# A hybrid S5 and gated-delta-rule layer on one core: a wide key norm, S5 setup queued behind the inputs, and the gate values computed later

## The chip, the cores and the metric

One core of a Trainium2 chip runs the whole layer in one launch. The metric is device time in microseconds, the median of several runs. The engines are TensorE (PE in the profile, its weight loads PEld), VectorE (DVE), ScalarE (ACT), GpSimd (POOL) and SyncE (SP), which issues most DMAs.

## The reference

One layer of a backbone on 1024 latent tokens and 256 context tokens, width 1024:

```
shift, scale, gate = split(silu(c) @ w_ada + b_ada)        # also for the context, from c_ctx
h = x * (1 + scale) + shift
u, z_s5, qkv, z_gdn, beta_l, alpha_l = split(h @ w_in)
S5 group (512 channels): diagonal complex state space, both directions, then GLU, times silu(z)
delta-rule group (4 heads of 128): q, k, v = silu(conv3x3(qkv)); q, k = l2norm(q), l2norm(k)
    beta = sigmoid(beta_l);  g = -exp(a_log) * softplus(alpha_l + dt_bias)
    chunked gated delta rule in both directions, gated RMS norm, times silu(z)
x_new = LN(alpha * x + gate * (concat(s5, gdn) @ w_out))
```

The key norm divides each key row of 128 by the root of its sum of squares plus 1e-6.

## The kernel before

The kernel is one long program; the framework takes the instructions in the order of the program as their priority, estimates when each is ready, and writes a fixed list for each engine. An instruction of low priority may so stand far ahead of its place in the program, in a hole of its engine. Each engine then runs its list in order, and a waiting instruction holds up what stands behind it. The block form `tc.issue_after(ins)` adds an edge from `ins` to the instructions in the block that are on the same engine as `ins`.

The front (`ada`, `hidden`, lines 509 to 572) goes over k = 0 to 7, the eight 128-wide slices of the width. `ada(k)` loads the x and context tiles and two 512 KB tiles `wad` of w_ada from SP's queue, and computes shift and scale (`pa`, `pas`, `ss`); `hidden(k)` transposes x on PE, scales it on ACT (`hraw`), splits it on DVE into `h_hi` and `h_lo`, and adds it to the u projection (`u_mm`). `s5_lam`, `s5_small` (line 240 on) compute powers of the S5 transition on small DVE tiles. `s5_load` (line 209) loads B, C (`bt`, `cnt`) and the skip weights into `spk`. `s5_mats` (line 370) forms the complex products of B, `s5_inject` (line 452) makes eight tiles `e` of products, three per tile on DVE and three on POOL for six of them, all six on DVE for two; PE transposes them, ACT copies them and they go to memory as `d_e`. `u_half` finishes the u projection in two halves. `e_stage` (line 613) loads `d_e` again and makes the chunk inputs `ebuf`; `fold` combines them on DVE, and `chain` is the sequential recurrence on POOL in three pieces, the second and third queued behind the key norm of heads 0 and 1 (`kpow`).

Between these stand, before the change, the values of beta and decay (`beta`, `lnb`, `gg`, `gx`, `ngx`): some 45 small DVE instructions, five on ACT and eight on PE. They are used first in `tbatch`, in the delta-rule part.

Then come four heads, each with three `conv_tile` calls (k, v, q): `proj` projects into PSUM banks of `psA` (four), ACT copies to `cr` and `ca`, DVE adds the taps, ACT applies SiLU, and for k and v PE transposes ten 128x128 blocks in groups of 4, 4 and 2 into PSUM banks of tag `w` (two banks; the function `bankE` gives the two of tag `e`). The buffers `ca` (tag `ac`) are two, shared by k, v and q. For k the groups are squared with a row sum on ACT (`jk`, `kss`), raised to -1/2 on POOL, multiplied on DVE into `ktk`, and transposed again (`pkT`). After head 1 stands `gate_stage`, which uses tag `e`. After the heads come the z projections, the S5 output, the GLU and the delta rule with the output projection.

Of the kernel before, what the change touches and what calls it, by code (L numbers as in the profile page):

```python
# [19 lines left out]
P = 128  # L20
# [21 lines left out]
def tile_hybrid_block(  # L42
# [462 lines left out]
    KS = 5  # L505
    pba = bankW("pba")
    xin = {}

    def ada(k):
        xk = hp.tile([P, 8, P], F32, tag=f"hh{k}", name=f"xk{k}")  # L510
        xc = hc.tile([P, 2, P], F32, tag=f"ch{k}", name=f"xc{k}")
        Q.dma_start(xk, x[0, :, k * P:(k + 1) * P].rearrange("(i p) f -> p i f", p=P))
        Q.dma_start(xc, cx[0, :, k * P:(k + 1) * P].rearrange("(i p) f -> p i f", p=P))
        wad = []
        for i in range(2):
            if k < 4:
                w = hp.tile([P, NK, P], F32, tag=f"h{'hl'[i]}{4 + k}", name=f"wad{k}_{i}")
            elif i:
                w = hp.tile([P, NK, P], F32, tag=f"hl{k}", name=f"wad{k}_{i}")
            else:  # L520
                w = c5([P, NK, P], f"wad{k}_{i}", ("kk", "ac")[k % 2])
            Q.dma_start(
                w, w_ada[0, :, i * D + k * P:i * D + (k + 1) * P].rearrange("(kt p) n -> p kt n", p=P),
            )
# [12 lines left out]
        pas = ld.tile([P, 256], F32, tag="pas", name=f"pas{k}", bufs=1)  # L537
        V.tensor_copy(pas, pa[:, :256])
        pm = pa[:, 256:260]
        for i in range(2):  # L540
            T.matmul(pm[:, 2 * i:2 * i + 2], pas[:, i * P:(i + 1) * P], sel, start=True, stop=True)
        ss = ld.tile([P, 4], F32, tag="ss", name=f"ss{k}")
        V.tensor_scalar(ss[:, 0:2], pm[:, 0:2], badd[:, k:k + 1], None, op0=ALU.add)
        V.tensor_scalar(ss[:, 2:4], pm[:, 2:4], badd[:, 8 + k:9 + k], 1.0, op0=ALU.add, op1=ALU.add)
        xin[k] = xk, xc, ss

    def hidden(k):
# [11 lines left out]
        h_hi[k] = hp.tile([P, LAT], F32R, tag=f"hh{k}", name=f"h_hi{k}")  # L559
        V.tensor_copy(h_hi[k], raw[:, :LAT])  # L560
        h_lo[k] = hp.tile([P, LAT], F32R, tag=f"hl{k}", name=f"h_lo{k}")
        V.tensor_tensor(h_lo[k], raw[:, :LAT], h_hi[k].bitcast(F32), op=ALU.subtract)  # L562
        c_hi[k] = hc.tile([P, CTX], F32R, tag=f"ch{k}", name=f"c_hi{k}")
        V.tensor_copy(c_hi[k], raw[:, LAT:])
        c_lo[k] = hc.tile([P, CTX], F32R, tag=f"cl{k}", name=f"c_lo{k}")
# [173 lines left out]
    def conv_tile(typ, hd):  # L739
# [44 lines left out]
        kt = c5([P, NT, P], "kt" + nm, "kk")  # L784
        if typ == 2:
            for i0, n4 in quads(NT):
                pv = bankW(f"pv{nm}_{i0}")
                for j in range(n4):
                    T.transpose(pv[:, j * P:(j + 1) * P], acc[:, (i0 + j) * P:(i0 + j + 1) * P], ident)
                S.activation(kt[:, i0:i0 + n4, :].rearrange("p j f -> p (j f)"), pv[:, :n4 * P], AF.Copy)  # L790
# [1 line left out]
            return  # L792
        kss = ld.tile([P, NT], F32, tag="kss", name=f"kss{hd}")
        for i0, n4 in quads(NT):
            pk = bankW(f"pk{nm}_{i0}")
            for j in range(n4):
                T.transpose(pk[:, j * P:(j + 1) * P], acc[:, (i0 + j) * P:(i0 + j + 1) * P], ident)
            for j in range(n4):
                jk = ld.tile([P, P], F32, tag="jk", name=f"jk{hd}_{i0}_{j}", bufs=1)
                S.activation(jk, pk[:, j * P:(j + 1) * P], AF.Square, accum_out=kss[:, i0 + j:i0 + j + 1])  # L800
            sl = slice(i0, i0 + n4)
            V.tensor_scalar(kss[:, sl], kss[:, sl], 1e-6, None, op0=ALU.add)  # L802
            kpow[hd] = G.tensor_tensor(kss[:, sl], kss[:, sl], mhalf[:, :n4], op=ALU.pow)  # L803
            V.tensor_tensor(
# [3 lines left out]
        S.dma_start(d_kt[hd], kt.rearrange("p j f -> p (j f)"))  # L808
        kT = c5([P, NT, P], "kT" + nm, "kk")
        for i0, n4 in quads(NT):  # L810
            pk = bankW(f"pkT{nm}_{i0}")
            for j in range(n4):
                T.transpose(pk[:, j * P:(j + 1) * P], kt[:, i0 + j, :], ident)
            S.activation(kT[:, i0:i0 + n4, :].rearrange("p j f -> p (j f)"), pk[:, :n4 * P], AF.Copy)
# [137 lines left out]
        for typ in (1, 2, 0):  # L952
            conv_tile(typ, hd)

    s5_load()
    bas = c5([P, 512], "bas", "kk")
    V.memset(bas, 0.0)
    for b, tn in enumerate((512, 512, 256)):
# [15 lines left out]
        for t in range(6):  # L974
            T.transpose(pcw[:, (6 * i + t) * 9:(6 * i + t + 1) * 9], cwn[:, t * P:(t + 1) * P], ident[:9, :9])
    V.tensor_copy(cwt.rearrange("p t a -> p (t a)"), pcw[:, :108])
    gr = per.tile([P, 2, 8], F32, name="gr")
    Q.dma_start(gr[:, 0, :], a_log.rearrange("o d h -> o (d h)").to_broadcast([P, 8]))
    Q.dma_start(gr[:, 1, :], dt_bias.rearrange("o d h -> o (d h)").to_broadcast([P, 8]))
    nea = sp.tile([P, 8], F32, name="nea")  # L980
    S.activation(nea, gr[:, 0, :], AF.Exp)
    V.tensor_scalar(nea, nea, -1.0, None, op0=ALU.mult)

    def gt(nm):
        return per.tile([P, 2, NT, HEADS], F32, name=nm)

    def dview(off):
        return gam[:, :, off:off + 8].rearrange("p n (d h) -> p d n h", d=2)

    def v4(t):  # L990
        return t.rearrange("p d n h -> p d (n h)")

    beta = gt("beta")
    for d in range(2):
        S.activation(beta[:, d], dview(0)[:, d], AF.Sigmoid)
    gtmp = ld.tile([P, 256], F32, tag="pas", name="gtmp", bufs=1)
    gtmq = ld.tile([P, P], F32, tag="jk", name="gtmq", bufs=1)
    ya, yb, yz = (gtmp[:, 80 * i:80 * i + 80].rearrange("p (d n h) -> p d n h", d=2, n=NT) for i in range(3))
    yq = gtmq[:, :80].rearrange("p (d n h) -> p d n h", d=2, n=NT)

    def softplus():
        V.tensor_scalar(yb, ya, -1.0, None, op0=ALU.mult)
        V.tensor_tensor(yb, ya, yb, op=ALU.min)
        S.activation(yb, yb, AF.Exp)
        V.tensor_scalar(yz, yb, 2.0, None, op0=ALU.add)
        V.reciprocal(yz, yz)
        V.tensor_mul(yz, yb, yz)
        V.tensor_mul(yb, yz, yz)
        V.tensor_scalar(yq, yb, 1.0 / 17, None, op0=ALU.mult)
        for cf in (1 / 15, 1 / 13, 1 / 11, 1 / 9, 1 / 7, 1 / 5, 1 / 3):  # L1010
            V.scalar_tensor_tensor(out=v4(yq), in0=v4(yq), scalar=cf, in1=v4(yb), op0=ALU.add, op1=ALU.mult)
        V.scalar_tensor_tensor(out=v4(yq), in0=v4(yq), scalar=1.0, in1=v4(yz), op0=ALU.add, op1=ALU.mult)
        V.tensor_scalar(ya, ya, 0.0, None, op0=ALU.max)
        V.scalar_tensor_tensor(out=v4(yq), in0=v4(yq), scalar=2.0, in1=v4(ya), op0=ALU.mult, op1=ALU.add)

    lnb = gt("lnb")
    for d in range(2):
        V.tensor_scalar(ya[:, d], dview(0)[:, d], -1.0, None, op0=ALU.mult)
    softplus()
    V.tensor_scalar(lnb, yq, -1.0, None, op0=ALU.mult)  # L1020
    for d in range(2):
        V.tensor_tensor(
            ya[:, d], dview(8)[:, d], bc(gr[:, 1, None, 4 * d:4 * d + 4], [P, NT, HEADS]), op=ALU.add,
        )
    softplus()
    gg = yb
    for d in range(2):
        V.tensor_tensor(gg[:, d], yq[:, d], bc(nea[:, None, 4 * d:4 * d + 4], [P, NT, HEADS]), op=ALU.mult)
    ghi = per.tile([P, 2, NT, HEADS], F32R, name="ghi")
    V.tensor_copy(ghi, gg)  # L1030
    ghf = ghi.bitcast(F32)
    glo = gt("glo")
    V.tensor_tensor(glo, gg, ghf, op=ALU.subtract)
    u_half(0)
    gx = per.tile([P, 2, 3, NT, HEADS], F32, name="gx")
    pgx = bankW("pgx")
    NC4 = NT * HEADS
    for d in range(2):
        for i, m in enumerate((tri[:, d, :], trir[:, d, :].bitcast(F32), ones)):
            o = (d * 3 + i) * NC4  # L1040
            T.matmul(pgx[:, o:o + NC4], m, gg[:, d].rearrange("p n h -> p (n h)"), start=True, stop=True)
    S.activation(gx.rearrange("p d i n h -> p (d i n h)"), pgx[:, :6 * NC4], AF.Exp)
    V.tensor_mul(gx[:, :, 1], beta, gx[:, :, 1])
    pgt = bankW("pgt")
    for d in range(2):
        T.transpose(pgt[:NC4, d * P:(d + 1) * P], gx[:, d, 0].rearrange("p n h -> p (n h)"), ident)
    grt = ld.tile([P, 256], F32, tag="pas", name="grt", bufs=1)
    V.tensor_copy(grt[:NC4], pgt[:NC4, :256])
    Q.dma_start(d_gr.rearrange("n h d p -> (n h) d p"), grt[:NC4].rearrange("p (d f) -> p d f", d=2))
    ngx = gt("ngx")  # L1050
    V.tensor_scalar(ngx, gx[:, :, 0], -1.0, None, op0=ALU.mult)
    s5_mats()
    s5_inject()
    u_half(1)
    pidx = sp.tile([P, 1], I32, name="pidx")
    G.iota(pidx, pattern=[[0, 1]], base=0, channel_multiplier=1)
# [621 lines left out]
```

## Time and profile before

| | us |
|---|---|
| median of 3 runs (range) | 923.16 (920.37 to 924.47) |
| profiled execution | 919.21 |
| its span | 917.5 |
| PE busy in the span | 814.1 (89%) |
| DVE busy | 672.5 (73%) |
| ACT busy | 415.2 (45%) |
| POOL busy | 392.1 (43%) |

The profile is one execution. Busy times count instructions in flight; PE's matmuls are pipelined, so that a busy PE isn't PE at its peak. The granted clock of PE is given beside it as a share of full speed, 0.949 over the span. An engine's idle time is put down to what ended it.

### The profile page before, as it was taken

The page shows a single profiled execution, that of the slowest core. Times are in us where ns is not written, and L with a number is a line of the kernel's source. Part 1 is how long each engine was busy: PE and PEld are TensorE (multiplying, and loading weights), DVE is VectorE, ACT ScalarE, POOL GpSimd, SP SyncE. Part 2 cuts the span into 40 slices and gives each one's busy share as a digit, 9 for nine tenths or more (in the row PEclk, how much of TensorE's full clock was granted, in tenths as well). Part 3 has the DMA queues.
Part 4 walks back from the last instruction along what each step waited for, and adds up shares of the span by engine and source line. Part 5 has one row for each costly group of instructions (what it writes and reads, how often), then busy time and mean ns, then how long its engine had stood idle before and what let it go on. Part 6 is the DMA issues. An engine that isn't in the chain of part 4 may idle for free. (4 is left out here: it accounts for less than half of the span.)

```text
span 917.5 us, 17187 instructions
## 1 busy us (share of the span) xinstructions
PE 814.1 (89%) x6553; PEld 674.8 (74%) x6553; DVE 672.5 (73%) x1318; ACT 415.2 (45%) x944; POOL 392.1 (43%) x463
## 2 busy tenths in 40 slices
PE   4988999997898999996899896899989889789994
PEld 2656897785786788874688674687988778678882
DVE  7988986996776778799573388567685585676686
ACT  1321435324434444431544376465763473556353
POOL 3215240007897940100311078874874485441163
PEclk9999999999798999998799897799999999999998
DMA  9981557412304232243454476421135234315332
GB/s 245 302 158 42 196 157 232 146 36 79 132 24 142 106 104 84 94 159 93 122 148 134 148 269 213 145 75 59 48 109 161 82 115 156 128 41 182 126 126 93
DMA packets 120125, 119.49 MB, mean 130 GB/s; under 512 B 21406, under 2 KB 95702, under 8 KB 119914
## 3 DMA queue, kind: packets, MB, share of 16 engines
q1 hardware_dynamic: 101946, 85.42, 32.7%
q10 hardware_dynamic: 18096, 32.97, 9.5%
q8 instruction: 51, 0.84, 0.4%
q14 instruction: 32, 0.26, 0.1%
HBM read 81.33 MB, written 37.04 MB: 129 GB/s over the span
## 5 line engine op out<-in xcount | busy, mean ns | idle before, releaser
L713 POOL TENSOR_TENSOR rta<-ebuf,ar 128x64 f32<-128x64 f32 x38 | 24.8, 653 | 85.3 <-DVE ebuf L688 82.6
L847 POOL COPY hq<-ebuf 64x1024 f32<-64x1024 f32 x8 | 16.4, 2068 | 93.9 <-DVE ebuf L688 58.5
L1187 POOL TENSOR_TENSOR mg<-tri,ghi 128x512 fp32r<-128x512 f32 x20 | 23.2, 1162 | 70.7 <-PE pd L1195 35.4
L1282 DVE TENSOR_TENSOR pad<-pp,lvm 128x256 f16<-128x256 f32 x100 | 40.5, 416 | 16.3 <-PE pp L1274 15.6
L141 PE MATMUL pjz<-h_hi,wtz 128*128 128x512 f32 x128 | 52.0, 406 | 0.1
L142 PE MATMUL pjz<-h_lo,wtz 128*128 128x512 f32 x128 | 52.0, 407 | 0.0
L143 PE MATMUL pjz<-h_hi,wtz 128*128 128x512 f32 x128 | 51.3, 401 | 0.0
L1298 PEld LDWEIGHTS <-xz 128*128 128x128 f16 x480 | 37.6, 101 | 18.5 <-issue 12.5
L1298 PE MATMUL px<-pad,xz 128*128 128x64 f16 x480 | 42.8, 198 | 7.0 <-DVE pad L1282 6.5
L1311 DVE TENSOR_TENSOR xz<-px,xz 128x512 f16<-128x512 f32 x60 | 40.6, 684 | 10.8 <-PE px L1298 8.8
L759 DVE SCALAR_TENSOR_TENSOR cak<-crk,cwt,cak 128x945 f32<-128x945 f32 (+2 forms) x32 | 39.3, 1229 | 7.3 <-ACT cak L749 6.9
L759 DVE SCALAR_TENSOR_TENSOR caq<-crq,cwt,caq 128x945 f32<-128x945 f32 (+2 forms) x32 | 39.2, 1224 | 7.2 <-ACT caq L749 5.3
L1298 PE MATMUL px<-xz,pad 128*128 128x64 f16 x480 | 42.8, 198 | 0.0
L759 DVE SCALAR_TENSOR_TENSOR cav<-crv,cwt,cav 128x945 f32<-128x945 f32 (+2 forms) x32 | 39.4, 1231 | 4.1 <-ACT cav L749 3.8
L1274 PE MATMUL pp<-xz,t 128*128 128x64 f16 x480 | 33.1, 197 | 7.1 <-DVE xz L1311 3.3
L803 POOL TENSOR_TENSOR kss<-kss,mhalf 128x4 f32<-128x4 f32 (+1 forms) x12 | 15.6, 1309 | 55.5 <-DVE kss L802 55.5
L1399 ACT ACTIVATE uu<-s 128x128 f32<-128x128 f32 x80 | 21.0, 275 | 38.7 <-PE s L1395 38.5
L1390 DVE SCALAR_TENSOR_TENSOR rr<-s,ngx,vt 128x128 f32<-128x128 f32 x72 | 24.5, 344 | 17.0 <-PE s L1386 16.4
L1274 PEld LDWEIGHTS <-t 128*128 128x128 f16 x480 | 27.5, 101 | 12.4 <-issue 10.4
L141 PE MATMUL u<-wu,h_lo 128*128 128x512 f32 x64 | 29.3, 458 | 5.5 <-DVE h_lo L562 5.5
L822 ACT ACTIVATE csz<-pjz 128x512 f32<-128x512 f32 x16 | 9.2, 597 | 54.9 <-PE pjz L143 43.0
L1395 PE MATMUL s<-rr,zf 128*128 128x128 f32 x144 | 31.4, 303 | 2.3 <-DVE rr L1390 1.8
(514 smaller groups left out, 3029.1 us busy)
## 6 DMA issues: line engine op xcount, KB each, us to landing
wad<-in_w_ada_dram SPq DMA_DIRECT2D x16, 512.0 KB, 6.3
xk<-in_x_dram SPq DMA_DIRECT2D x8, 512.0 KB, 6.5
d_e<-et ACTq DMA_DIRECT2D x8, 512.0 KB, 2.8
etl<-d_e SPq DMA_DIRECT2D x8, 512.0 KB, 4.3
wg<-in_w_ada_dram SPq DMA_DIRECT2D x8, 512.0 KB, 5.7
wrz<-in_w_in_dram SPq DMA_DIRECT2D x8, 512.0 KB, 3.9
d_z<-csz ACTq DMA_DIRECT2D x8, 512.0 KB, 2.9
xr<-in_x_dram SPq DMA_DIRECT2D x8, 512.0 KB, 5.4
```

What stands on the lines that cost most here:

```text
L141: T.matmul(ps, ll, rh, start=first, stop=False)
L142: T.matmul(ps, lh, rl, start=False, stop=False)
L143: return T.matmul(ps, lh, rh, start=False, stop=last)
L713: G.tensor_tensor(ta, prev, ar, op=ALU.mult)
L759: clast[typ, hd] = V.scalar_tensor_tensor(out=o, in0=rv[:, y0 + dy:y1 + dy, x0 + dx:x1 + dx], scalar=cwt[:, t, (dy + 1) * 3 + dx + 1:(dy + ...
L1187: G.tensor_tensor(mg[:, i], bc(tri[:, 0:2, None, :], [P, 2, 2, P]), bc(gsrc[:, :, c0:c0 + 2, hd, None], [P, 2, 2, P]), op=ALU.mult,)
L1274: T.matmul(pp[:, u * 64:(u + 1) * 64], t16[:, u, :], cols(xs[u], b, u // 2), start=True, stop=True)
L1282: V.tensor_tensor(scat(pad[:, 0, :], b, 256, 128 // b), pp[:, :256].rearrange("p (d n b) -> p d n b", d=2, b=b), lvm[:, l - 1].rearrange(" ...
L1298: ins = T.matmul(o, lt, rt, start=not on_act, stop=not on_act or w == 3 and i == 1)
L1311: V.tensor_tensor(xo, pxv, xo, op=ALU.add)
L1390: V.scalar_tensor_tensor(out=rn, in0=p1_[:, :P], scalar=ngx[:, d, ch, hd:hd + 1], in1=rr, op0=ALU.mult, op1=ALU.add,)
L1395: ins = T.matmul(p2_[:, :P], hs["zf"][cp][:, d, i, :], rr, start=True, stop=True)
```

## The change

Four edits. The loads of `s5_load` are queued on SP behind the last `wad` load. The DVE instructions of `s5_mats` and `s5_inject` are queued behind the last `h_lo`. The block that computes beta and decay stands after `head(1)` instead of before `s5_mats`; its text is the same, but `nea` is in another pool. In `conv_tile` the row sums of squares come from one ACT square over the whole group into `kt` and a DVE reduction, and the third group of each set of transposes takes a bank of tag `e`.

```diff
+            front["wad"] = Q.dma_start(w, w_ada[...])
...
+        front["lo"] = V.tensor_tensor(h_lo[k], raw[:, :LAT], h_hi[k].bitcast(F32), op=ALU.subtract)
...
-                pv = bankW(f"pv{nm}_{i0}")
+                pv = (bankE if i0 == 8 else bankW)(f"pv{nm}_{i0}")
...
-            pk = bankW(f"pk{nm}_{i0}")
+            pk = (bankE if i0 == 8 else bankW)(f"pk{nm}_{i0}")
...
-            for j in range(n4):
-                jk = ld.tile([P, P], F32, tag="jk", name=f"jk{hd}_{i0}_{j}", bufs=1)
-                S.activation(jk, pk[:, j * P:(j + 1) * P], AF.Square, accum_out=kss[:, i0 + j:i0 + j + 1])
             sl = slice(i0, i0 + n4)
+            S.activation(kt[:, sl, :].rearrange("p j f -> p (j f)"), pk[:, :n4 * P], AF.Square)
+            V.tensor_reduce(out=kss[:, sl], in_=kt[:, sl, :], axis=AX.X, op=ALU.add)
             V.tensor_scalar(kss[:, sl], kss[:, sl], 1e-6, None, op0=ALU.add)
...
-            pk = bankW(f"pkT{nm}_{i0}")
+            pk = (bankE if i0 == 8 else bankW)(f"pkT{nm}_{i0}")
...
-    s5_load()
+    with tc.issue_after(front["wad"].ins):
+        s5_load()
...
-    gr = per.tile([P, 2, 8], F32, name="gr")
...
     u_half(0)
-    s5_mats()
-    s5_inject()
+    with tc.issue_after(front["lo"].ins):
+        s5_mats()
+        s5_inject()
     u_half(1)
...
     for hd in range(HEADS):
         head(hd)
+        if hd == 1:
+            gr = per.tile([P, 2, 8], F32, name="gr")
...
         if hd < 2:
             with tc.issue_after(kpow[hd].ins):
```

## Rows read from the trace of the kernel before

**Rows 1.** Stages: busy (count) of PE, PEld, DVE, ACT, POOL, then PEclk, DMA, GB/s.
```profile
44.00:92.00 48.00, 40.56 (x286) 28.44 (x287) 40.87 (x92) 12.53 (x19) 17.39 (x12) 0.93 0.53 107
92.00:137.40 45.40, 45.40 (x240) 42.42 (x238) 40.15 (x89) 19.27 (x41) 16.68 (x11) 1.00 0.51 177
137.40:222.80 85.40, 83.60 (x579) 66.57 (x576) 74.63 (x105) 30.12 (x57) 11.00 (x14) 1.00 0.44 127
222.80:247.00 24.20, 15.40 (x82) 13.39 (x80) 13.09 (x15) 13.91 (x39) 19.47 (x36) 0.78 0.32 116
247.00:300.00 53.00, 49.09 (x237) 38.58 (x237) 36.90 (x39) 21.09 (x49) 45.45 (x71) 0.91 0.29 100
```

**Rows 2.** Waits of PE: who waited for whom, us in total, times, longest.
```profile
PE pkk L797 <- DVE ktk L804: 9.6, 2, 5.7
```

**Rows 3.** Timeline of SP's queue, 36 to 70 us: start, duration, what it issued.
```profile
44.98 5.55 SPq L213 DMA_DIRECT2D bt<-in_s_b_re_dram  x2
...
51.83 1.40 SPq L512 DMA_DIRECT2D xk<-in_x_dram  x1
...
66.09 0.38 SPq L512 DMA_DIRECT2D xk<-in_x_dram  x1
66.56 0.53 SPq L522 DMA_DIRECT2D wad<-in_w_ada_dram  x1
```

**Rows 4.** Timeline of DVE in the front.
```profile
76.27 1.77 DVE L407 TENSOR_TENSOR e<-e,e1v 128x512 f32<-128x512 f32 x1
77.97 2.12 DVE L562 TENSOR_TENSOR h_lo<-hraw,h_hi 128x1024 fp32r<-128x1024 f32 x1
80.01 1.77 DVE L406 TENSOR_TENSOR e2v<-spk,ep 128x512 f32<-128x512 f32 x1
81.70 0.41 DVE L538 COPY pas<-pa 128x256 f32<-128x256 f32 x1
```

**Rows 5.** Timeline of PE in the front (k = 5, then k = 7).
```profile
72.68 0.63 PE L142 MATMUL u<-wu,h_hi 128*128 128x512 f32 x1
...
88.73 0.60 PE L141 MATMUL u<-wu,h_lo 128*128 128x512 f32 x1
89.17 0.41 PE L142 MATMUL u<-wu,h_hi 128*128 128x512 f32 x1
```

**Rows 6.** Touching spk (DVE, POOL); POOL's products; last product; touching gtmp (PE, PEld, DVE, ACT).
```profile
44.00:88.25 44.25, 11.22 (x13) 10.74 (x9) 0.92 0.57 116
...
L408 POOL TENSOR_TENSOR e<-spk,ep 128x512 f32<-128x512 f32 x2 | 2.6, 1336 | 0.1
...
132.41 0.68 DVE L410 TENSOR_TENSOR e<-e,e7g 128x512 f32<-128x512 f32 x1
...
92.00:122.00 30.00, 1.43 (x12) 1.42 (x12) 13.77 (x42) 0.54 (x2) 1.00 0.52 181
```

**Rows 7.** The key norm: timelines of PE and POOL, then groups of ACT and DVE.
```profile
229.59 0.66 PE L797 MATMUL pkk<-ident,cak 128*128 128x128 f32 x2 [5.70 <-DVE ktk L804]
278.34 0.66 PE L797 MATMUL pkk<-ident,cak 128*128 128x128 f32 x2 [3.91 <-DVE ktk L804]
...
227.38 0.32 POOL L716 TENSOR_TENSOR ebuf<-rta,rtb 128x64 f32<-128x64 f32 x1
227.65 1.04 POOL L803 TENSOR_TENSOR kss<-kss,mhalf 128x4 f32<-128x4 f32 x1
276.45 2.00 POOL L803 TENSOR_TENSOR kss<-kss,mhalf 128x4 f32<-128x4 f32 x2
...
L800 ACT ACTIVATE jk<-pkk 128x128 f32<-128x128 f32 x40 | 11.1, 278 | 10.8 <-PE pkk L797 10.0
L800 ACT ACTIVATION_READ_ACCUMULATOR jk<-pkk 128x1 f32 x40 | 7.9, 198 | 0.0
L1004 ACT ACT_TABLE_LOAD x1 | 1.3, 1283 | 0.1
L804 DVE TENSOR_TENSOR ktk<-pkk,kss 128x512 f32<-128x512 f32 (+1 forms) x12 | 7.2, 600 | 13.3 <-POOL kss L803 13.3
```

More of the change, by code (lines that the diff above doesn't have):

```diff
@@ L507, in tile_hybrid_block @@
     xin = {}
+    front = {}
     def ada(k):
@@ L521, in ada @@
                 w = c5([P, NK, P], f"wad{k}_{i}", ("kk", "ac")[k % 2])
-            Q.dma_start(
+            front["wad"] = Q.dma_start(
                 w, w_ada[0, :, i * D + k * P:i * D + (k + 1) * P].rearrange("(kt p) n -> p kt n", p=P),
@@ L561, in hidden @@
         h_lo[k] = hp.tile([P, LAT], F32R, tag=f"hl{k}", name=f"h_lo{k}")
-        V.tensor_tensor(h_lo[k], raw[:, :LAT], h_hi[k].bitcast(F32), op=ALU.subtract)
+        front["lo"] = V.tensor_tensor(h_lo[k], raw[:, :LAT], h_hi[k].bitcast(F32), op=ALU.subtract)
         c_hi[k] = hc.tile([P, CTX], F32R, tag=f"ch{k}", name=f"c_hi{k}")
@@ L976, in tile_hybrid_block @@
     V.tensor_copy(cwt.rearrange("p t a -> p (t a)"), pcw[:, :108])
-    gr = per.tile([P, 2, 8], F32, name="gr")
[L978 to L1033, printed above, removed]
-    u_half(0)
[L1035 to L1049, printed above, removed]
@@ L1050, in tile_hybrid_block @@
-    ngx = gt("ngx")
-    V.tensor_scalar(ngx, gx[:, :, 0], -1.0, None, op0=ALU.mult)
-    s5_mats()
-    s5_inject()
+    u_half(0)
+    with tc.issue_after(front["lo"].ins):
+        s5_mats()
+        s5_inject()
     u_half(1)
@@ L1104, in tile_hybrid_block, with gt, dview, v4 @@
         head(hd)
+        if hd == 1:
+            gr = per.tile([P, 2, 8], F32, name="gr")
+            Q.dma_start(gr[:, 0, :], a_log.rearrange("o d h -> o (d h)").to_broadcast([P, 8]))
+            Q.dma_start(gr[:, 1, :], dt_bias.rearrange("o d h -> o (d h)").to_broadcast([P, 8]))
+            nea = per.tile([P, 8], F32, name="nea")
+            S.activation(nea, gr[:, 0, :], AF.Exp)
+            V.tensor_scalar(nea, nea, -1.0, None, op0=ALU.mult)
+            def gt(nm):
+                return per.tile([P, 2, NT, HEADS], F32, name=nm)
+            def dview(off):
+                return gam[:, :, off:off + 8].rearrange("p n (d h) -> p d n h", d=2)
+            def v4(t):
+                return t.rearrange("p d n h -> p d (n h)")
+            beta = gt("beta")
+            for d in range(2):
+                S.activation(beta[:, d], dview(0)[:, d], AF.Sigmoid)
+            gtmp = ld.tile([P, 256], F32, tag="pas", name="gtmp", bufs=1)
+            gtmq = ld.tile([P, P], F32, tag="jk", name="gtmq", bufs=1)
+            ya, yb, yz = (gtmp[:, 80 * i:80 * i + 80].rearrange("p (d n h) -> p d n h", d=2, n=NT) for i in range(3))
+            yq = gtmq[:, :80].rearrange("p (d n h) -> p d n h", d=2, n=NT)
+            def softplus():
+                V.tensor_scalar(yb, ya, -1.0, None, op0=ALU.mult)
+                V.tensor_tensor(yb, ya, yb, op=ALU.min)
+                S.activation(yb, yb, AF.Exp)
+                V.tensor_scalar(yz, yb, 2.0, None, op0=ALU.add)
+                V.reciprocal(yz, yz)
+                V.tensor_mul(yz, yb, yz)
+                V.tensor_mul(yb, yz, yz)
+                V.tensor_scalar(yq, yb, 1.0 / 17, None, op0=ALU.mult)
+                for cf in (1 / 15, 1 / 13, 1 / 11, 1 / 9, 1 / 7, 1 / 5, 1 / 3):
+                    V.scalar_tensor_tensor(out=v4(yq), in0=v4(yq), scalar=cf, in1=v4(yb), op0=ALU.add, op1=ALU.mult)
+                V.scalar_tensor_tensor(out=v4(yq), in0=v4(yq), scalar=1.0, in1=v4(yz), op0=ALU.add, op1=ALU.mult)
+                V.tensor_scalar(ya, ya, 0.0, None, op0=ALU.max)
+                V.scalar_tensor_tensor(out=v4(yq), in0=v4(yq), scalar=2.0, in1=v4(ya), op0=ALU.mult, op1=ALU.add)
+            lnb = gt("lnb")
+            for d in range(2):
+                V.tensor_scalar(ya[:, d], dview(0)[:, d], -1.0, None, op0=ALU.mult)
+            softplus()
+            V.tensor_scalar(lnb, yq, -1.0, None, op0=ALU.mult)
+            for d in range(2):
+                V.tensor_tensor(
+                    ya[:, d], dview(8)[:, d], bc(gr[:, 1, None, 4 * d:4 * d + 4], [P, NT, HEADS]), op=ALU.add,
+                )
+            softplus()
+            gg = yb
+            for d in range(2):
+                V.tensor_tensor(gg[:, d], yq[:, d], bc(nea[:, None, 4 * d:4 * d + 4], [P, NT, HEADS]), op=ALU.mult)
+            ghi = per.tile([P, 2, NT, HEADS], F32R, name="ghi")
+            V.tensor_copy(ghi, gg)
+            ghf = ghi.bitcast(F32)
+            glo = gt("glo")
+            V.tensor_tensor(glo, gg, ghf, op=ALU.subtract)
+            gx = per.tile([P, 2, 3, NT, HEADS], F32, name="gx")
+            pgx = bankW("pgx")
+            NC4 = NT * HEADS
+            for d in range(2):
+                for i, m in enumerate((tri[:, d, :], trir[:, d, :].bitcast(F32), ones)):
+                    o = (d * 3 + i) * NC4
+                    T.matmul(pgx[:, o:o + NC4], m, gg[:, d].rearrange("p n h -> p (n h)"), start=True, stop=True)
+            S.activation(gx.rearrange("p d i n h -> p (d i n h)"), pgx[:, :6 * NC4], AF.Exp)
+            V.tensor_mul(gx[:, :, 1], beta, gx[:, :, 1])
+            pgt = bankW("pgt")
+            for d in range(2):
+                T.transpose(pgt[:NC4, d * P:(d + 1) * P], gx[:, d, 0].rearrange("p n h -> p (n h)"), ident)
+            grt = ld.tile([P, 256], F32, tag="pas", name="grt", bufs=1)
+            V.tensor_copy(grt[:NC4], pgt[:NC4, :256])
+            Q.dma_start(d_gr.rearrange("n h d p -> (n h) d p"), grt[:NC4].rearrange("p (d f) -> p d f", d=2))
+            ngx = gt("ngx")
+            V.tensor_scalar(ngx, gx[:, :, 0], -1.0, None, op0=ALU.mult)
```

## The prediction

> **What bounds the kernel now.** I read the busy time by stage first, then who waited for whom on PE, then the queues' own timelines in the stretches where PE loses time. By stage [rows 1], PE is the busiest engine. It loses time in three places that the change touches. From 44 to 92 us it is busy 40.56 of 48 and the granted clock is 0.93 of full speed: 7.4 us idle, and 0.07 x 48 = 3.4 us lost to the lower level, 10.8 in all. From 92 to 222.8 it is as good as full. From 222.8 to 247 it is busy 15.40 of 24.2 at 0.78: 8.8 idle and 5.3 lost to the clock. From 247 to 300 it is busy 49.09 of 53 at 0.91: 3.9 idle, 4.8 lost. After a wait the clock is at the lower of its two levels (1.2 and 2.4 GHz) for a while: a 512-column matmul shows 0.63 us there and 0.41 at the higher one [rows 5].
>
> The first loss is in the front, where x is scaled into h_hi/h_lo. SP issues x and w_ada tiles in its own order, and the S5 loads of s5_load stand ahead of the last of them: the first two of the four bt loads take SP 5.55 us from 44.98 on, the x tile of k = 6 follows at 51.83, and the x tile and the last w_ada tile of k = 7 only at 66.09 and 66.56 [rows 3]. DVE then has the S5 products between the steps of k = 6 and 7, and they are slow because POOL works on its own products beside them: 1.77 us for a 128x512 product that takes 0.68 at 132.41 when POOL is idle [rows 4, 6]. h_lo of k = 6 takes 2.12 us, and the copy pas of k = 7, which starts the chain to h_lo of k = 7, leaves DVE only at 81.70 [rows 4]. The matmuls of k = 7 begin at 88.73 [rows 5].
>
> The second and third losses are one wait: the third group of key transposes (tile pkk, line 797) waits for ktk, 9.6 us in two times [rows 2], 5.70 in head 0 and 3.91 in head 1 [rows 7]. It needs the PSUM bank that the first group gives back after the square, the power on POOL and the multiply on DVE.
>
> **The change, part by part.** The sum is made against the profiled execution, 919.21 us (span 917.5, 1.7 around it); the median of the runs shown is 923.16, 3.95 above it.
>
> *S5 loads behind the last w_ada load.* Twelve DMAs leave the middle of the input stream. Two of them alone hold SP 5.55 us. With them gone the x tile of k = 7 can follow that of k = 6 [rows 3]. The loads then land after the inputs; their first user is the product that now waits for h_lo of k = 7, so they have the time of two k steps. Behind them on SP come conv_w and the projection weights, first needed when u_half is done.
>
> *S5 products behind h_lo of k = 7.* The block edges hold each engine's own instructions; those of s5_mats and s5_inject on DVE are held, and POOL's follow by their data. Up to 88 us DVE spends 11.22 us and POOL 10.74 on instructions that touch spk [rows 6]; with the few that touch only m or e added, and the copies of s5_small and the selects taken off, I take 14 us on DVE and 11 on POOL that leave the front (estimates). What remains for PE there is its own work and the short chain pa, pas, ss, hraw, h. I take 8 of the 10.8 us; the ends are 3 (only the waits on h_lo go) and 10.8. This moves everything behind it forward if nothing of the moved work is late.
>
> The moved work must not be late either. Between 92 and 122 us DVE spends 13.77 us on instructions that touch gtmp, the tile of beta and decay [rows 6]; these leave that stretch. So DVE gains 14 and loses 14 behind h_lo: the last product, now ending at 133.1 [rows 6], should end at about 125, with PE having u_half and its transposes to do until about 129 (137.4 less 8). The cover is 4 us thin, and if it goes each us shows one for one in e_stage.
>
> On the two engines side by side the trace shows 1.77 for 0.68 [rows 4, 6]. The Trainium skill ("SBUF — State Buffer", Who interferes with whom) says that a Vector instruction with two SBUF inputs and a GpSimd one that reads SBUF take one shared pair in turn, the second waiting for the first. By that rule the two engines' products add up instead of overlapping, which speaks against packing them all behind h_lo: rival 3 is that case; the forecast takes the overlap that 92 to 137.4 us had.
>
> *Beta and decay chain behind head 1.* Its work is unchanged, some 14 us on DVE, 8 small PE instructions, a few on ACT. Its inputs are there by 92 to 122 us, where it runs now, so it may be put into any hole of DVE before 300 (DVE is busy 36.9 of 53 at 247 to 300, [rows 1]); its users are in the delta-rule part long after. I cost it at 0 on PE. If the cover is gone, the 14 us delay convolution taps, one for one. On ACT it splits a stretch that had one function table: a table load is 1.28 us [rows 7], and at most four more come, 5 us on an engine that is under 50% busy, 1 us on the path.
>
> The Trainium skill ("ScalarE: Activation LUTs", Table sets: the hidden batching unit) asks to batch calls by table set and prices each switch at about 2.7 us, which speaks against this place. By it four switches would be 10.8 us of ACT, still beside PE's work; by the row 5.
>
> *Wide key norm.* Forty pairs of square and accumulator read of 128 columns (11.1 us and 7.9 busy, overlapping to about 0.4 us each pair) become twelve wide squares, which I price like the twelve ktk multiplies of the same shapes, 7.2 us in all [rows 7]: ACT saves about 9 us. DVE gets twelve tensor_reduces of up to 128x512 that the trace does not show; by the same row I take 7 us in all; from below the bound is half of that, from above twice. From 247 on DVE has room; head 0's 1.6 us fall where DVE is idle waiting for the power. The norm's latency hardly changes: 1.6 us of squares become 0.6 plus a reduce of about 0.6.
>
> *Third group in a bank of the other tag.* The wait of 5.70 and 3.91 goes. It freed more than the bank: the third transposes also give back cak, whose buffer caq needs, and through caq's copies PE's accumulators. What is late next is the power. It stands in POOL's queue behind a piece of the S5 chain: in head 0 the first piece's last instruction starts at 227.38 and the power at 227.65; in head 1 the power of two groups runs at 276.45 in the same place, behind the second piece [rows 7]. So ktk of the first group cannot be earlier, and the pkT transposes behind the third group will wait for it unless matmuls stand between. In head 0, 24 context matmuls of 256 columns can (at most 24 x 0.41 / 2 = 4.9 us, by half of a 512-column one, [rows 5]). So of 14.1 us lost there (8.8 and 5.3) I take back 5; the ends are 1 (transposes directly behind) and 14. In head 1 the loss is 8.7; the second piece of the chain starts sooner by the third group's wait, PE comes sooner too: I take 2, ends 0 and 8.7.
>
> Bank tag e is shared with gate_stage, which holds one bank from its first matmul to pgs; there are two, so I cost this at 0, and up to 5 if both are taken at once.
>
> The sum: 8 + 5 + 2 - 1 = 14 off 919.2, 905 on the scale of the profiled execution, 909 on that of the median.
>
> **The rivals.**
> 1. *The stalls go altogether*: the list puts enough matmuls between the third group and pkT, and the front is bound by PE alone. Then about 25 of the 33.6 us (10.8 + 14.1 + 8.7) come back: 894, on the median's scale 898 (891 to 900). For it: PE has projections of the next tiles waiting. Against: POOL's chain ends when it ends.
> 2. *DVE gives the front's gain back*: from 137.4 to 222.8 us DVE is busy 74.63 of 85.4 and PE 83.60 [rows 1], both near full; if DVE sets when the S5 fold ends, and the beta chain's 14 us land in this stretch, POOL's chain and so the power come no sooner, PE just waits longer at the norm. Gain 0 to 3: 920 to 923 on the median's scale (917 to 925). For it: the power runs right behind the chain in both heads [rows 7]. Against: the fold's inputs come from PE, which is ahead.
> 3. *The S5 products end late*: DVE and POOL take turns. DVE has 30 inject products and 6 of s5_mats, 36 x 0.68 = 24.5; POOL 18 at 1.34 or more [rows 6], 24; one after the other 48.5 us, and DVE's copies of u, bas and weights, some 12 (an estimate: what is left of its 40.15 us at 92 to 137.4 [rows 1] without beta and the products), between them. From 80 that ends at 140, 7 later than 133.1. Then e_stage, the fold, the chain and the power are 7 later each, PE idles where it was full, at half clock afterwards (3 more), and the front's gain is gone: 919.2 + 10 - 3 for the bank = 926, 930 on the median's scale (926 to 936). It decides when the last product of e ends after 133.1. Against: the products from 88 to 133 shared both engines too and PE did not wait for them.
>
> **How the numbers follow.** This kernel's runs tell about 0.5% from no change, 918.5 to 927.8. Forecast (900 to 917): 0.54. Rival 1: 0.17. Rival 2: 0.16. Rival 3: 0.10. The remaining 0.03 lies at both ends: the whole order of the list may shift. Predicted is the forecast's 909. The range leaves out rival 3 and the lowest ends: 891 to 925. Faster: 0.54 + 0.17 and a little of rival 2, 0.72; same: most of rival 2 and the edge of rival 3, 0.16; slower 0.12.
>
> **What would show it.** Front right: the x and w_ada tiles of k = 7 issued before any bt, and PE's first matmul on h_lo of k = 7 near 81 instead of 88.73; wrong if still past 86. Products in time: the last write of e before 133.1, and PE full up to e_stage. Norm right: no wait of pkk for ktk; what is left appears as pkTk waiting for ktk, under 5 us per head. Beta chain harmless: no convolution tap waits behind it. The prediction is wrong if 222.8 to 247 shows as much idle PE as before, or if a new wait of PE on e, u or the e-tag banks appears.

## The result and the profile after

The changed kernel takes 926.06 us, the kernel before 921.72 (medians of 13 runs each); the ratio is 1.0052, 95% interval 1.0034 to 1.0070: 0.5% slower, where 909 was forecast. The profiled execution of after took 929.01 us (span 927.3), that of before 919.21. Of these 9.8 us, 1.1 come up to the first state matmul (`s`) of the delta-rule part (595.3 us before, 596.5 after), 9.4 between it and the last output matmul (`pout`), and 0.7 are gained behind it. The profiled execution of after is the slowest of its 13 runs, and that of before lies 2.5 us under its median: the 9.8 us are more than twice the difference of the medians, 4.3.

By stage, with the same cuts and columns as [rows 1]:

```profile
44.00:92.00 48.00, 44.27 (x322) 32.55 (x323) 36.32 (x113) 17.10 (x30) 6.86 (x8) 0.96 0.56 116
92.00:137.40 45.40, 41.11 (x192) 37.39 (x191) 44.18 (x76) 13.00 (x30) 23.22 (x17) 0.99 0.49 170
137.40:222.80 85.40, 82.36 (x562) 67.12 (x560) 72.17 (x104) 30.93 (x56) 4.97 (x6) 0.97 0.40 120
222.80:247.00 24.20, 19.39 (x103) 16.16 (x102) 18.60 (x23) 10.33 (x19) 23.03 (x35) 0.93 0.28 104
247.00:300.00 53.00, 47.86 (x250) 39.45 (x249) 42.91 (x46) 22.57 (x36) 50.49 (x71) 0.97 0.29 97
```

The front gained: 44.27 us of PE instead of 40.56. The next stage gave it back: PE, full before, is idle 4.3 us, with POOL at 23.22 instead of 16.68. From 222.8 to 247, the norm's stage, PE is 4 us busier; from 247 to 300 it is 1.2 us less busy. SP's queue, PE and DVE after (against [rows 3, 5, 6]):

```profile
52.86 0.42 SPq L513 DMA_DIRECT2D xk<-in_x_dram  x1
53.37 2.08 SPq L523 DMA_DIRECT2D wad<-in_w_ada_dram  x1
55.50 7.53 SPq L213 DMA_DIRECT2D bt<-in_s_b_re_dram  x2
```

```profile
80.93 0.61 PE L141 MATMUL u<-wu,h_lo 128*128 128x512 f32 x1
```

```profile
124.65 0.23 DVE L1090 TENSOR_TENSOR glo<-gtmp,ghi 128x80 f32<-128x80 f32 x1
...
137.72 0.69 DVE L410 TENSOR_TENSOR e<-e,e7g 128x512 f32<-128x512 f32 x1
```

The inputs of k = 7 go first, its matmuls begin at 80.93 instead of 88.73, and yet the last S5 product stands at 137.72 instead of 132.41. Between them the end of the beta and decay chain, `glo`, stands at 124.65: in DVE's list it did not leave the products, though its text moved behind head 1. What touches its tile gtmp (columns PE, PEld, DVE, ACT), after:

```profile
92.00:126.00 34.00, 0.00 (x0) 0.00 (x0) 19.25 (x38) 0.54 (x2) 1.00 0.47 162
```

Before, the 42 instructions took 13.77 us, 0.33 each [rows 6]; now 38 take 19.25, 0.51 each (four more run just before 92). The mean hides two kinds of rows: beside a POOL product a small DVE instruction ends when that product ends, and without one it takes about 0.24 us:

```profile
117.76 1.61 POOL L410 TENSOR_TENSOR e<-e,e4g 128x512 f32<-128x512 f32 x1
118.16 1.32 DVE L1071 SCALAR_TENSOR_TENSOR gtmq<-gtmq,gtmp 128x80 f32<-128x80 f32 x1
121.71 1.28 POOL L410 TENSOR_TENSOR e<-e,e5g 128x512 f32<-128x512 f32 x1
121.72 1.33 DVE L1087 CAST ghi<-gtmp 128x80 fp32r<-128x80 f32 x1
...
112.93 0.23 DVE L1068 SCALAR_TENSOR_TENSOR gtmq<-gtmq,gtmp 128x80 f32<-128x80 f32 x1
```

Of the chain's 36 instructions with 128x80 operands, 11 run almost wholly beside POOL's after and take 1.01 us in the mean; before there were four (0.97). PE's waits after (total, times, longest):

```profile
PE pkTk L813 <- DVE ktk L804: 9.2, 3, 5.1
...
PE poa L141 <- DVE y L1528: 4.3, 3, 2.2
PE pkk L1217 <- DMA kT<-d_qkv: 4.3, 2, 2.3
```

The wait of [rows 2] is gone and pkTk waits in its place, as forecast. The wait for the load of kT is in the delta-rule part, which the change doesn't touch.

### The profile page after: what moved, and what is told of

The parts are those of the page before. It is cut to its first block, busy times and chain, and to the rows that moved or that the text cites. A ratio compares the mean times of both kernels' runs of the same rounds, so it can differ in the third digit from the quotient of the medians.

```text
span 927.3 us, 17125 instructions
## 1 busy us (share of the span) xinstructions
PE 822.8 (89%) x6553; PEld 677.6 (73%) x6553; DVE 677.7 (73%) x1330; ACT 410.1 (44%) x878; POOL 384.0 (41%) x463
## 5 line engine op out<-in xcount | busy, mean ns | idle before, releaser
L1312 ACT ACTIVATE xz<-px 128x512 f16<-128x512 f32 x40 | 23.6, 595 | 22.9 <-PE px L1301 17.3
L1412 DVE SCALAR_TENSOR_TENSOR st<-st,gx,s 128x128 f32<-128x128 f32 x64 | 21.4, 343 | 16.4 <-PE s L1405 15.7
L1528 DVE SCALAR_TENSOR_TENSOR y<-xr,poa 128x512 f32<-128x512 f32 x16 | 11.0, 688 | 29.8 <-PE poa L143 19.4
```

Source lines behind the costliest of these rows:

```text
L1312: S.activation(xo, pxv, AF.Copy)
```

## The experiments

Each kernel was timed in five rounds beside the kernel before on the same chip; ratios are to it. "Before + ..." and "after + ..." say what is edited. Columns: start of the last S5 product `e`, start of the last product with `a8i` in the unfold (the S5 part's last step on DVE, which ends 1.2 to 1.7 us later), first `s`, time from first `s` to last `pout` (all four from one profiled execution each, us), and the ratio with its 95% interval.

| | e | unfold | s | s to pout | ratio |
|---|---|---|---|---|---|
| before | 132.4 | 439.0 | 595.3 | 309.0 | 1 |
| after | 137.7 | 439.9 | 596.5 | 318.4 | 1.0052 (1.0034 to 1.0070) |
| e1 norm, bank | 134.0 | 436.9 | 593.7 | 308.9 | 0.9951 (0.9924 to 0.9979) |
| e2 two edges | 137.5 | 440.1 | 594.0 | 308.4 | 0.9965 (0.9939 to 0.9991) |
| e3 block moved | 134.8 | 457.5 | 618.8 | 311.4 | 1.0167 (1.0132 to 1.0203) |
| e4 after, chain held | 129.8 | 440.7 | 595.7 | 314.2 | 1.0016 (0.9990 to 1.0043) |
| f1 after, block back | 137.4 | 435.6 | 591.8 | 311.7 | 0.9959 (0.9939 to 0.9979) |
| f2 norm, edges | 137.4 | 440.7 | 594.6 | 321.6 | 1.0117 (1.0087 to 1.0147) |
| f3 after, no bank | 135.8 | 447.6 | 606.7 | 307.5 | 1.0089 (1.0065 to 1.0113) |
| f4 norm, bank, load | 136.6 | 439.1 | 594.5 | 317.6 | 1.0050 (1.0029 to 1.0071) |
| g1 block after head 0 | 135.3 | 436.1 | 592.5 | 308.2 | 0.9974 (0.9948 to 1.0000) |
| g2 kT first | 136.6 | 439.3 | 593.5 | 318.6 | 1.0053 (1.0025 to 1.0082) |
| g3 chain behind unfold | 129.6 | 429.1 | 620.7 | 307.0 | 1.0224 (1.0192 to 1.0256) |
| g4 g3 without edges | 135.2 | 434.8 | 626.3 | 307.4 | 1.0300 (1.0259 to 1.0342) |
| k1 g3, block cut | 129.2 | 428.6 | 599.2 | 309.5 | 1.0028 (1.0004 to 1.0053) |
| k2 k1, no product edge | 135.8 | 438.1 | 606.2 | 307.6 | 1.0101 (1.0061 to 1.0141) |
| k3 before, block cut | 135.0 | 447.9 | 611.5 | 315.2 | 1.0197 (1.0162 to 1.0231) |
| m1 chain late | 132.3 | 434.8 | 593.8 | 310.8 | 0.9934 (0.9907 to 0.9962) |
| m2 chain late, pgx later | 129.9 | 429.4 | 586.8 | 313.1 | 0.9917 (0.9889 to 0.9945) |

m1 and m2 have the same lists up to some 480 us, and their unfolds still end 5.4 us apart: a difference of that size before 440 between two single profiles proves nothing.

**First the parts.** The theory then was the late last product.

```diff
e1: before + wide square and tensor_reduce, bankE for the third groups
e2: before + both issue_after blocks (front["wad"], front["lo"])
e3: before + the beta and decay block behind head(1)
```

> The kernel before with the wide key norm and the third group in a bank of tag e alone; front, S5 products and beta chain as before. Theory (place: the loss is the late last e product, which the edges and the beta chain make together): front milestones as before (last e product near 132, POOL chain's start near 211), no pkk wait for ktk, last q tap of head 3 some 5 us before 388.8, and 2 to 5 us faster than before, ratio 0.994 to 0.998. Rival A (the norm's gain is always lost in the DVE-bound unfold that follows): last q tap earlier, end of unfold at 439 as before, ratio 0.998 to 1.002. Rival B (the twelve reduces cost DVE more than the bank saves): ratio over 1.002.

> The kernel before with the two S5 edges alone (loads behind the last w_ada load, products behind h_lo of k=7); beta and decay at their old place, norm as before. Theory (place): first matmul on h_lo of k=7 near 81, last e product 136 to 139, POOL chain's start 216 to 219, pkk still waits for ktk; slower than before by 4 to 9 us, ratio 1.004 to 1.010. Rival A (the products are late for nothing, the loss of the changed kernel comes from the new place of the beta chain in the delta-rule part): ratio 0.993 to 1.002 though the last e product is late.

> The kernel before with the beta and decay block behind head 1 alone; no edge, norm as before. Theory (place): most of the chain's DVE instructions stand between the taps of heads 1 and 2 (about 240 to 310 us), the last e product ends earlier than 133 (118 to 126), e_stage still begins near 137 because PE is full until then, the POOL chain starts at 205 to 211; ratio 0.994 to 1.001. Rival A (the new place itself costs: taps wait for the chain, or the delta-rule part gets a worse list): ratio 1.003 or more, with the loss either at the last q tap (after 389) or behind 595 us.

e1 came as the theory had it. e2 did not: its last product is as late as after's, and it is faster than before all the same. e3 is slow by 1.67%, and its loss lies at the taps: the block, one instruction between two taps, ends only at 330. It drags along what stands behind it in the program: the last `pga` matmuls of the gate stage run at 343.78 (305.95 before), and have waited for weights on the way.

```profile
240.00:335.00 95.00, 1.43 (x12) 1.49 (x12) 10.52 (x33) 0.27 (x1) 0.98 0.25 85
```

```profile
305.95 1.05 PE L895 MATMUL pga<-wg,cond 128*32 128x512 f32 x4
...
343.78 1.92 PE L895 MATMUL pga<-wg,cond 128*32 128x512 f32 x4 [1.23 <-DMA wg<-in_w_ada_dram]
```

```profile
340.00:360.00 20.00, 14.32 (x48) 7.42 (x47) 6.48 (x10) 6.81 (x27) 3.67 (x3) 0.57 0.18 66
```

The first row (e3, what touches gtmp) shows 33 of the chain's instructions among the taps of heads 0 to 2; the last (e3, all work) PE busy 14.32 of 20 us at a granted clock of 0.57, full at 1.00 before. So the same block, moved alone, does leave the S5 products; with the edges it does not. The products held back open holes where the list puts what is ready.

```diff
e4: after, the block in: with tc.issue_after(clast[0, 1].ins):   # last q tap of head 1
```

> The changed kernel with the beta and decay block's DVE instructions held behind the last q tap of head 1, so that they cannot fill holes among the S5 products. Theory (place: the chain stayed among the products and made the last of them 5 us late): last e product 124 to 129, e_stage as soon as PE is done with u (near 130), POOL chain's start 203 to 209, no long pkT wait in head 0; 8 to 16 us faster than the changed kernel, ratio to before 0.985 to 0.996. Rival A (DVE and POOL take turns on the products, the beta chain only fills what they leave): last e product 134 or later, POOL chain's start 214 or later, ratio to before 1.002 to 1.008. Rival B (front regained, but the DVE-bound unfold or the delta-rule part gives it back): POOL chain near 205, end of unfold at 438 to 440, ratio 0.998 to 1.006.

It came as rival B. The chain is gone from the products, and e_stage's first matmul moves from 134.5 to 126.6, but between the taps of heads 1 and 2 it costs as much, and the unfold comes no sooner (440.7, after 439.9). What touches gtmp in e4:

```profile
92.00:126.00 34.00, 0.00 (x0) 0.00 (x0) 0.00 (x0) 0.00 (x0) 1.00 0.55 181
270.00:330.00 60.00, 1.43 (x12) 1.44 (x12) 12.68 (x42) 0.54 (x2) 0.97 0.33 104
```

**Then the delta-rule part.** After and e4 have the same order of instructions there on PE, another than before and e2 (which share one), though no line of it is edited: the list is planned from estimated times, and a small shift ahead changes it. Call after's order D.

```diff
f1: after, block back at its old place
f2: f1 without bankE                     # order D
f3: after without bankE
f4: e1 + the edge on the S5 loads only   # order D
```

> The changed kernel with the beta and decay block back at its old place: both edges, the wide norm and the bank of tag e remain. Theory L (two losses, both by the list: the moved block's small instructions cost some us up to 595, and the delta-rule part got another order of instructions that is 5 us longer; norm with bank 0.9951 and edges 0.9965 add up): this kernel's order of the delta-rule part is neither that of before nor that of the changed kernel; from first s to last pout 307 to 311 us instead of the changed kernel's 318, first s near 591 to 593, ratio 0.988 to 0.994. Rival A (the gains don't add: both need the same room on DVE before 440): ratio 0.995 to 1.000. Rival B (norm and edges together make the loss): ratio over 1.002.

> Both edges and the wide norm, beta and decay at the old place, all transposes in banks of tag w. Its list of the delta-rule part is the same as that of the changed kernel. Theory L: first s to last pout 314 to 318 us, pkk waits for ktk as before, ratio 0.997 to 1.004. Rival A (the delta-rule part's extra length in the changed kernel comes from the moved block's data or is chance of one profile): first s to last pout 307 to 311, ratio 0.991 to 0.997.

> The changed kernel with all transposes in banks of tag w; its order of the delta-rule part is that of the kernel with the beta block alone moved, which took 311.4 us from first s to last pout. Theory L: 308 to 312 there; up to first s the bank's gain is gone, so 598 to 602; ratio 1.001 to 1.006. Rival A (the delta-rule part is longer wherever the block is moved): 314 to 318 there, ratio 1.007 to 1.012. What the bank is worth follows from first s and the last q tap against the changed kernel.

> Wide norm, bank of tag e and the edge of the S5 loads alone; no edge for the products, beta and decay at the old place. Its order of the delta-rule part is that of the changed kernel. Theory L: 314 to 318 us from first s to last pout, so ratio 0.995 to 1.003 although the front gains. Rival A (that order costs nothing): 307 to 311 there, ratio 0.987 to 0.994. For the front both say: h_lo of k=7 ends some 4 to 8 us before 87, last e product before 132.4.

The four kernels with D took 314.2 to 321.6 us from first `s` to last `pout`; before and the ten others whose order is that of before, e1, e3, f1 or g3 took 307.0 to 311.7. The boundary moves a little in this: in D 21 PE instructions stand behind the first `s` that stand before it in the kernel before (2,921 against 2,900; 2,906 at most in the eleven). From the first `pd` (the delta-rule part's first decay matmul, behind which all have 3,336) the four take 375.6 to 382.3 and the eleven 370.0 to 374.1, so the two groups stay apart, by less. The granted clock doesn't explain it: from `s` to `pout` it is 0.979 in after and 0.983 in before and g1. f2 and f4 move no block and are slow there; f3 moves it and is not. f2's ratio lies beyond what either theory gave. f1 came as rival A: the gains do not add up, 0.9959 where e1 and e2 together would give 0.992. f4 against e1 shows D's price best: they differ by the edge on the loads alone, reach `s` 0.8 us apart, and the ratios are 1.0050 and 0.9951, 9 us. For f4 the front's forecast was wrong: with the edge on the loads alone h_lo of k=7 starts at 89.7 (87.0 before), and the ratio lies above both ranges. f3 against after shows the bank's worth up to `s`: 10 us, more than I wrote, so f3's ratio missed the theory's range although its `s` to `pout` came as it said.

```diff
g1: after, "if hd == 1:" of the block -> "if hd == 0:"
g2: after, with tc.issue_after(kT_load): the load of kt
```

> The changed kernel with the beta and decay block behind head 0 instead of head 1. DVE's list is the same up to the taps of head 1, the chain still stands among the S5 products; the order of the delta-rule part is no longer D (the one that the changed kernel, e4, f2 and f4 share: 314 to 322 us from first s to last pout) but the one of e3 and f3 (311.4 and 307.5). Theory D (the order D costs some 8 us, and nothing else makes the changed kernel slower than before): first s within 3 us of 596.5, first s to last pout 306 to 312, ratio 0.993 to 0.999. Rival A (what the changed kernel loses hangs on its other edits, the order of the delta-rule part only goes along): ratio 1.003 to 1.008.

> The changed kernel with one edge on SP: in the delta-rule part a head's load of kt is queued behind its load of kT (in the order D kt goes first, and PE waits 3.2 to 5.6 us for kT). PE's list before the delta-rule part is unchanged; within it part of the order changes too. Theory E (of what D costs, about half is these two waits): no wait of pkk for the kT load over 0.5 us, first s to last pout 311 to 316, ratio 0.999 to 1.003. Rival A (the load is not what costs, PE would wait for something else): 316 to 319, ratio 1.004 to 1.007.

g1 is the changed kernel with the block one head earlier; DVE's list is the same into the taps of head 1, the chain stands where it stood in after, and the kernel is 0.78% (1.0052 to 0.9974, some 7 us) faster. Not all of that is the order: g1's first `s` stands 4.0 us before after's, where the theory allowed 3. By stage, before, after and g1:

```profile
660.00:720.00 60.00, 55.74 (x586) 49.23 (x585) 39.12 (x92) 27.60 (x86) 33.38 (x40) 0.97 0.37 121
...
840.00:920.00 80.00, 62.77 (x333) 51.51 (x331) 50.66 (x143) 34.36 (x96) 24.53 (x25) 0.93 0.37 126
```

```profile
660.00:720.00 60.00, 53.64 (x560) 45.48 (x559) 37.97 (x88) 29.74 (x90) 32.47 (x42) 1.00 0.42 135
...
840.00:920.00 80.00, 72.04 (x453) 59.77 (x448) 55.71 (x164) 39.92 (x113) 22.29 (x25) 0.99 0.36 120
```

```profile
660.00:720.00 60.00, 56.28 (x603) 50.25 (x601) 41.39 (x95) 28.79 (x89) 31.52 (x39) 0.97 0.43 133
...
840.00:920.00 80.00, 59.02 (x298) 47.94 (x297) 49.29 (x139) 31.97 (x89) 24.52 (x24) 0.93 0.34 115
```

In after, PE issues fewer instructions from 660 to 720 and has 453 left for the last stretch (298 in g1). g2 takes the wait for kT away and PE then waits for others (0.6 us for kT, 4.3 in after; 4.7 now for `on`; 318.6 from `s` to `pout`): that load was not the cause, theory E fell.

```profile
PE po L1443 <- DVE on L1442: 4.7, 3, 3.7
...
PE pkk L1218 <- DMA kT<-d_qkv: 0.6, 1, 0.6
```

Which dependence makes D slow stays open. Nor is PE's order the only thing that goes with D: the lists of DVE, ACT, POOL and SP differ there too.

**Last, can the forecast's gain be had?** The theory: the chain's 14 us of DVE must stand where nothing urgent is behind them.

```diff
g3: after, block behind unfold(), DVE held by its last carry
g4: g3 without the two edges
```

> The changed kernel with the beta and decay block behind the unfold in the program and its DVE instructions held behind the unfold's last one, where DVE has holes (437 to 445 us and 482 to 505). Theory (the chain among the S5 products makes the last e product late, and its other places cost taps): last e product 127 to 131 as in e4, POOL chain's start 208 to 211, last tap ends 380 to 385 (386.2 without the move), first s 586 to 590; the order of the delta-rule part is a new one close to that of before, 307 to 312; ratio 0.987 to 0.993. Rival A (the earlier chain is worth nothing, DVE bounds the taps and the unfold): last tap and first s as without the move (386, 592), ratio 0.994 to 0.998. Rival B (the chain comes too late for the delta-rule part): first pd later than 536, first s after 596, ratio over 1.000.

> Wide norm and bank of tag e with the beta and decay block held behind the unfold, no edge on the S5 loads and products. Theory: without the chain the products end earlier than before (last e product 118 to 126 instead of 132 to 134), e_stage begins when PE is done with u near 137, POOL chain's start 206 to 211; first s 588 to 592, ratio 0.990 to 0.995. Rival A (the products end where the S5 loads and POOL let them, near 132): as e1, first s 593 to 594, ratio 0.994 to 0.998. Against g3 it tells what the two edges are worth once the chain is out of the way: by the theory 1 to 4 us, by the forecast's 8 us of front 6 to 8.

In g3 the front's gain reaches the end of the unfold, 429.1 instead of 439.0, and is lost on the spot. By its numbers that is rival B, but the chain is not late for the delta-rule part: PE's list has the chain's matmuls ahead of the z projections, SP's the write of d_gr ahead of a load of u.

```profile
PE pgx L1112 <- DVE gtmp L1100: 18.2, 1, 18.2
PE py L854 <- DMA u<-d_ug: 13.9, 1, 13.9
```

g4 has the same wait for gtmp (18.2 us) and missed both its ranges. Up to the unfold g4 is 5.7 us behind g3; k1 and k2 below tell better what the edges give.

```diff
k1: g3, the block cut after glo; the rest (gx, pgx, pgt, d_gr, ngx) behind y_stage(1), held on PE
k2: k1 without the edge on the products
k3: before + the cut block as in k1
```

> All edits of the change, but the beta and decay block is cut in two: its DVE part (to glo) held behind the last DVE instruction of the unfold, its matmuls, gx, the write of d_gr and ngx behind the second S5 output tile on PE. Its order of the delta-rule part is that of the kernel before. Theory (the forecast's 14 us are there once the chain fills no hole among the products and nothing waits for it): unfold ends near 429, no wait of PE for gtmp over 1 us, first pd 520 to 525, first s 583 to 587, first s to last pout 307 to 311; 905 to 911 us, ratio 0.981 to 0.988. Rival A (PE or the loads bound 437 to 530, the unfold's gain is not passed on): first s 590 to 594, ratio 0.994 to 0.998. Rival B (the chain still delays somebody, ACT's Exp or the mg products): first s after 596, ratio over 1.000.

> k1 without the edge that queues the S5 products behind h_lo of k=7; same order of the delta-rule part. Theory (the edge on the products makes the front's gain, the load edge alone makes none, as in f4 where h_lo of k=7 stood at 89.7): first matmul on h_lo of k=7 near 91, unfold ends 434 to 437, 4 to 8 us slower than k1, ratio to before 0.987 to 0.993. Rival A (with the chain gone DVE has room for the products in the front, so the edge is worth nothing): within 2 us of k1.

> The kernel before with the block cut and placed as in k1, no other edit. Its order of the delta-rule part is a new one. Theory (the chain's place alone frees 14 us of DVE among the products, but PE is busy with u to 137, so little comes of it without the edges): last e product 128 to 134, POOL chain's start 209 to 212, unfold ends 436 to 440, first s 592 to 596; ratio 0.994 to 1.001 if its order of the delta-rule part costs nothing (307 to 312 from first s to last pout). Rival A (the chain's place is what costs in all kernels, the edges nothing): unfold ends near 431, ratio 0.986 to 0.992.

The theory missed. k1 has the wait gone and the unfold at 428.6, but its S5 output takes 80.5 us from first to last `py`, 66.0 before: the chain's 16.41 us (gtmp, 425 to 455) now stand ahead of the products `f`.

```profile
425.00:455.00 30.00, 0.00 (x0) 0.00 (x0) 16.41 (x42) 0.54 (x2) 0.69 0.35 97
```

k2 is 0.7% slower than k1: that much the product edge gives once the chain is away; k3 shows that the new place alone gains nothing (last tap ends at 400, 391 before; why, with no chain among the taps, was not traced).

```diff
m1: k1, DVE part held behind the last instruction of s5_toeplitz (t3), the rest behind y_stage(2)
m2: m1, the rest behind y_stage(3)
```

> k1 with the block's DVE part held behind the last DVE instruction of the last S5 output products (the toeplitz stage), its matmuls, gx, the write of d_gr and ngx behind the third S5 output tile. Theory (the chain costs its 14 us wherever DVE has urgent work behind it, and here it has none): unfold ends near 429, first to last py 64 to 70 us, first s 581 to 586; 900 to 909 us, ratio 0.977 to 0.986, if the order of the delta-rule part (a new one) takes 307 to 312 from first s to last pout, 5 to 8 us more if it is as dear as D. Rival A (the chain is now late for the delta-rule part): first pd more than 86 us behind the last product of the unfold's end, first s 590 to 598. Rival B (the S5 output is bound by PE, loads or ACT): first to last py over 75 us, ratio 0.993 to 1.000.

> m1 with the chain's matmuls, gx, the write of d_gr and ngx behind the fourth S5 output tile instead of the third. Same up to 480 us. Theory: first s within 3 us of m1; what differs behind it is the order of the delta-rule part alone. Rival A (gx comes too late for the first batch): first s 4 us or more behind m1's.

Both beat both kernels: 915.69 and 914.09 us, 0.66 and 0.83% under before. That is less than the theory's 900 to 909, and m1's `s` and ratio lie in its rivals' ranges. `s` came later than I wrote since I took 86 us from the unfold's end to the first `pd`; before needs 93.7, m2 94.1, m1 95.8. m2's `s` lies 7 us before m1's, outside the 3, and 5.4 of these stand there at the unfold already. m1's and m2's ratios overlap, so which place of pgx is better is not told. In m2 (first) DVE takes the chain here, where before (second) has room; columns as in [rows 1]:

```profile
480.00:500.00 20.00, 20.00 (x130) 17.75 (x129) 14.07 (x42) 12.74 (x16) 2.43 (x2) 1.00 0.55 166
500.00:520.00 20.00, 17.01 (x64) 13.00 (x63) 7.64 (x16) 7.82 (x12) 1.21 (x2) 0.83 0.41 131
```

```profile
480.00:500.00 20.00, 20.00 (x204) 16.66 (x203) 9.16 (x17) 9.51 (x10) 4.03 (x2) 1.00 0.45 129
500.00:520.00 20.00, 15.61 (x84) 13.28 (x83) 6.91 (x9) 8.59 (x12) 0.00 (x0) 0.83 0.57 194
```

PE stays full at 480 to 500 with DVE 4.9 us busier.

## Why the prediction was wrong, step by step

*Loads and front: right in the mechanism.* The inputs of k = 7 go ahead of every bt, PE is there at 80.93, forecast 81. It takes the products' edge: with that on the loads alone h_lo of k = 7 is no earlier (f4). Of the forecast's 8 us the two edges alone bring 0.35% (interval 0.09 to 0.61%), 3.2 us (e2).

*Products in time: the first step that failed.* "these leave that stretch" is wrong. The program's place is only a priority; the products' edge opened holes in DVE's list, and the chain, ready early, stayed in them. The last product ended at 138.4, not 125. With the chain held out it ended at 129.9 to 130.5 (e4, g3, k1, m2) and 133.0 (m1), so 5 to 8.5 of the 13.4 us are the chain's. The rest is rival 3's mechanism, which the sum left out: in e4 the 35 products that DVE still has behind h_lo of k = 7 take 35.6 us, at 0.68 each they would be 24; 13 of them run beside POOL and take over 1 us. The Trainium skill ("SBUF — State Buffer", Who interferes with whom) has Vector and GpSimd take one pair in turn, the second waiting; the trace agrees, the chain's 0.24 us becoming 1.32 and 1.33 where POOL's product ends just before. But rival 3's point of decision was no such point: e2 is past it (138.2), and is faster than before. That the median came out at the 926 where rival 3's range begins is chance.

*Beta and decay chain: "I cost it at 0 on PE" failed.* Alone it cost 1.67% (e3), held among the taps it took back the front (e4), behind the unfold 14 us (k1). DVE has idle time in sum at 247 to 300, but the chain stands among the taps there, and the gate stage behind it comes late (e3). e4 is near rival 2, DVE giving the front's gain back, though at 286 to 322 us and not at 137 to 223. Of the places tried it costs least behind the last S5 products, where DVE was busy 9.16 and 6.91 of 20 us before (m1, m2).

*Norm and bank: right.* Forecast 5 + 2 = 7 (the 1 taken off is the chain's table loads), measured 0.49% (interval 0.21 to 0.76%), 4.5 us (e1). The waits moved to pkTk, 5.1 at the longest, just over the 5 that I allowed. But this gain and that of the front don't add up: both together bring 0.41% (f1), even without the block's move.

*The order of the list: mis-sized.* I gave 0.03 to "the whole order of the list may shift". It did, over 200 us behind the last edited instruction (the taps and norm of head 3 end at 390), and it is the larger part of the loss: 9.4 of the 9.8 us between the two profiles (8 if counted from the first `pd`), 9 between e1 and f4, and at most 7 by g1, whose `s` is earlier too. That the order causes it, and not what else changes with it, is shown as far as four kernels against eleven do. Without it the change would have been about as fast as before or 0.26% faster (g1, interval up to 1.0000), not 1.5%: the rest of the forecast's 14 us is missing by the steps above, of which m2 gets back 8.5 us in all (922.59 to 914.09).

## What to carry to other kernels

Where a list is planned by priority and estimated times, moving code does not move its instructions: look up in the new list where they went, and hold them by an edge where it matters. A chain of small instructions is cheap only where its engine has idle time and nothing urgent behind it; hold the engines that wait for it (PE's matmuls, the queue's write) as well, or they stop everything behind them. Compare the planned order of parts that were not edited too, since a shift there can cost more than the edit gives.

## What was not expected

The order of the engines' lists (2,900 PE instructions among them), with the same work, went with 5 to 13 us more in a stretch of 309 us (4 to 11 from the first `pd`). A small DVE instruction (128x80) took about 0.24 us alone and up to 1.33 beside one POOL product: what it cost was not its own length but what was left of POOL's.
